# A decoder step on one core: second half's attention outputs of layer 1 kept in DRAM as fp32, and Winograd weight sums of layer 1 made by VectorE

## The chip, the core and the metric

The kernel runs on one core of one Trainium2 chip. The metric is the device time of one execution in microseconds, lower is better. Matrix products run on TensorE (PE in the profile; PEld are its weight loads), element-wise work on VectorE (DVE) and ScalarE (ACT), and DMAs are issued from the queues of SyncE (SP) and GpSimd (POOL).

## The reference, cut to what matters

A two-layer decoder trunk handles a prompt of 1024 tokens and eight sample tokens with the same weights (model width 1024, 4+4 heads of 128, feed-forward width 2816). Layer 0 mixes with a gated linear recurrence and attention into 256 memory tokens; layer 1 with stick-breaking attention over one shared K/V and memory attention. Each layer ends with a SwiGLU, and every sub-layer is normed on both sides:

```python
def swiglu(h, w_gu, w_down):
    gate, up = jnp.split(h @ w_gu, 2, axis=-1)
    return (jax.nn.silu(gate) * up) @ w_down
...
        else:
            mix = b_mixer(hn, w_in_b[l - N_A], sb_bias[l - N_A], k_all, v_all, q_pos, k_pos, ...)
        h = h + rmsnorm(mix, g[1])
        h = h + rmsnorm(swiglu(rmsnorm(h, g[2]), w_gu[l], w_down[l]), g[3])
```

Everything is fp32.

## The kernel before, in words

**Halves and precision.** The tokens are worked on in two halves: half 0 has 512 prompt tokens, half 1 has 512 and the eight sample tokens (520 columns). Activations lie transposed, 128 features on the partitions, tokens along the row; a half is eight such tiles `x[k]`. A fp32 product is made of three products of rounded parts: `split_to` (L226) and `split_w` (L192 on) write a high part with ScalarE (L206, L227) and the rest with VectorE (L207, L228). `proj` (L211) multiplies eight weight tiles of 128x128 with the eight `x[k]` into a bank of PSUM (L220).

**Plain and Winograd blocks.** The feed-forward width is cut into 22 blocks of 128, in five parts of 5, 5, 4, 4 and 4 (`PARTS`). For each part the gate and up products of its blocks come first, then its way down: eight row tiles (`w_down`), added to the result `R`. `ffn.part` does this plainly. `ffn_w` does it for half 1 of layer 1 (`f1`) and in two other places: its first blocks are plain too, with two banks per product (`gate_up_q`, L452 on, products L464), and beside them `sums_w` (L277 on) makes sums of `x` (L298, L306); its other blocks (`gate_up_w`, L481 on) need seven products of half the tokens and half the rows instead of eight, a Winograd scheme (products L511). Each of the seven needs one 512x128 weight, split at L501/L502; four of the seven weights are sums of two to four quarters of `w_gu`. For `f1` blocks 0 to 2 are plain and 19 are Winograd blocks. The products end in four PSUM banks, each held once, so a bank must be evacuated (L518 to L535) before the next block's product into it.

**Where the weight sums come from.** `weight_sums` (L545 on) forms four sums per part in DRAM with plain and accumulating DMAs of 256 rows from GpSimd's queue, 16 per part; a one-column copy (L563) holds each of them until the other work is as far as the weave wants. For layer 1 that is `ws`, 80 DMAs, woven into the stages from layer 0's memory attention on to the output projection of half 1. `gate_up_w` then loads each of the seven weights with one DMA (L496) from `w_gu` or from a sum.

**Order.** The work is written as generators that `weave` interleaves by given weights; what the tile framework makes of it is a fixed order on every engine, and each engine runs its own in that order. Buffers are taken from pools in turn (`wraw` 5 raw weights, `wspl` 5 split weights, `bpool` 7 rows of 512, `tpool` 3, `npool` 2). Towards the end the stages are:

1. Attention of half 1 in layer 1 (`b1.sb`, `b1.mem`, and the sample's attentions), woven with parts 0, 1, 2 of half 0's plain feed-forward and with the four gate/up steps of its part 3 (`p3`). Each head's output `po` is split into `xo[k]`, a tile with both parts (L912 and L1405); the sample's eight columns are added at L959.
2. The output projection of half 1, `o1.mm` (384 products), woven with the last `ws`.
3. `o1.finish`: norm (`rstd_from`, its products are L256), residual (L381, L387), a second norm, and `normed` (L273, L228), which makes the `x` of `f1`; woven with the rest of `p3`, its way down, and part 4.
4. `f1.part(0)` and `part(1)`, woven with the end of half 0 (`f0.finish`, also L381, L387, and the transposes of `store_y`, L1453), then parts 2, 3 and 4. The way down of `ffn_w` is L648 with its evacuations at L655 and L657.

Of the kernel before, what the change touches and what calls it, by code (L numbers as in the profile page):

```python
# [18 lines left out]
P = 128  # L19
# [4 lines left out]
def tile_decoder(  # L24
# [201 lines left out]
    def split_to(dst, src):  # L226
        nc.scalar.copy(dst[0], src)  # L227
        nc.vector.tensor_sub(dst[1], src, dst[0].bitcast(F32))  # L228

    def silu(dst, ps, g):  # L230
# [251 lines left out]
    def gate_up_w(g, l, f, ops, spl, raws):  # L482
# [4 lines left out]
        gate, up = f * P, DFF + f * P  # L487
        src = [
            (w_gu[l][0:512, gate : gate + P], 0), (sums[l][part][0][:, o : o + P], 4), (sums[l][part][1][:, o : o + P], 5),
            (w_gu[l][512:D, gate : gate + P], 1), (sums[l][part][2][:, o : o + P], 6), (sums[l][part][3][:, o : o + P], 2),  # L490
            (w_gu[l][512:D, up : up + P], 3),
        ]
# [12 lines left out]
        def product(ps, j, first=False):  # L505
            w = split(weight(j))
            i = src[j][1]
            for k in range(4):
# [66 lines left out]
    class ffn_w:  # L575
# [288 lines left out]
    def mem_attn(g, l, qm, xo):  # L864
# [4 lines left out]
        for h in range(H):  # L869
            po = S()  # L870
            for pr in range(2):
# [38 lines left out]
                yield  # L910
            d = xo[H + h]
            split_to((d[:, 0, :G], d[:, 1, :G]), po)  # L912

# [25 lines left out]
    def sample_pv(pT, load, xo, k0):  # L939
# [15 lines left out]
        for h in range(H):  # L955
            nc.tensor.transpose(pr[:, h * NB : (h + 1) * NB], ot[:NB, h * P : (h + 1) * P], ident[:NB, :NB])
        for h in range(H):
            d = xo[k0 + h]
            split_to((d[:, 0, G : G + NB], d[:, 1, G : G + NB]), pr[:, h * NB : (h + 1) * NB])  # L959
        yield  # L960
# [379 lines left out]
    def sb_prompt(g, Qs, xo):  # L1340
# [49 lines left out]
        for h in range(H):  # L1390
# [12 lines left out]
            values(vh, po, *late)  # L1403
            d = xo[h]
            split_to((d[:, 0, :G], d[:, 1, :G]), po)  # L1405

# [17 lines left out]
    class mixer_b:  # L1424
# [6 lines left out]

        def open(self):
            self.xo = wo_tiles(self.g)

# [117 lines left out]
    weave((a1.sample(), 6), (a1.gate(), 4), (f0.part(1), 9), (w0, 9))  # L1552
    ws = weight_sums(1, range(5))

# [8 lines left out]

    weave((chain(a1.merge(), a1.mem()), 30), (a1.mem_sample(), 50), (rest(), 24), (islice(ws, 2), 6))
    xk0, xb0 = [], []
# [6 lines left out]
    b0 = mixer_b(0, xb0)  # L1572
    weave((b0.heads(), 8), (o1.finish(), 17), (islice(ws, 4), 4))
    b0.open()
    f1 = ffn(1, 0, o1.x)
    weave((chain(b0.sb(), b0.mem()), 25), (chain(f1.part(0), f1.part(1)), 18), (islice(ws, 34), 35))
    set_banks(True)
    fw = ffn_w(1, 0, o1.x, (5, 6, 5), 2, False, f1.R)
    weave((chain(fw.part(2), fw.part(3), fw.part(4)), 24), (islice(ws, 8), 8))
    f1.acc = fw.acc  # L1580
# [5 lines left out]
    weave((normed(1, f1.R, f1.r, gkvcol, xk1, True), 8), (o0.mm(b0.xo, 5, 7), 2))  # L1586
    weave((kv_proj(1, xk1), 8), (islice(ws, 10), 11))
    weave((normed(1, f1.R, f1.r, lambda k: gcol(1, 0, k), xb1), 8), (o0.mm(b0.xo, 7, ND), 1))
    b1 = mixer_b(1, xb1)
    weave((b1.heads(), 8), (o0.finish(), 17), (islice(ws, 8), 9))  # L1590
    b1.open()
    f0 = ffn(0, 1, o0.x)
# [44 lines left out]
```

## Time and profile before

| | |
|---|---|
| timed runs | 2450.82 us median of 3 (2448.91 to 2453.11) |
| the profiled execution | 2446.43 us |
| its span, first to last instruction | 2444.6 us |
| mean granted TensorE clock | 0.999 |
| moved by DMA | 397.42 MB, mean 163 GB/s |
| the chain that ended last | PE 87%, DVE 6%, DMA 3%, rest under 3% each |

The page of the profile gives busy times for the whole span; stages are read from windows of it. A row of a window has the stretch, its length, then for each engine the busy time and the number of instructions, the granted clock, the share of the DMA engines and GB/s. A row of the groups has line, engine, operation, tiles, shapes and count, then busy time and mean ns of one, then the engine's idle time before them and what ended it. A row of the timeline has start, length, engine, line, operation, tiles and count, and in brackets the idle time before it. Line numbers are those of the kernel before; in the changed kernel they lie 8 to 45 lines later.

### The profile page before, as it was taken

Reading aid. Unit: us, or ns where it says so; the run is one execution under the profiler, and the core shown is the slowest. Engines: PE = TensorE matmul, PEld = TensorE weight load, DVE = VectorE, ACT = ScalarE, POOL = GpSimd, SP = SyncE. Lnnn points to the kernel's source line nnn. Section 1 sums busy time; section 2 is a strip of 40 time slices with the busy share of each in tenths; the row PEclk is TensorE's granted clock in tenths of the full one; section 3 lists DMA queues with packets and bytes.
Section 4 is the critical chain, followed back from the end, with each engine's and each line's share of the span. In section 5 each row is a group of like instructions: output and inputs, shape, how many; then the busy total and the mean of one; then the engine's idle time right before and its main releaser. Section 6 shows DMA issues by size and latency. Waiting matters only on the chain.

```text
span 2444.6 us, 42106 instructions
## 1 busy us (share of the span) xinstructions
PE 2412.0 (99%) x15839; PEld 2159.3 (88%) x15839; DVE 1639.0 (67%) x2987; ACT 1251.2 (51%) x2441; POOL 186.1 (8%) x315
## 2 busy tenths in 40 slices
PE   8999999999999999999999999999999999999998
PEld 6888888888889988999999989877777888999998
DVE  5867557665897686654756686777788467755565
ACT  5547544344445555554434554555555445654445
POOL 1001101101000000111200102121000100000000
PEclk9999999999999999999999999999999999999999
DMA  5454666577746447677766649655354563464542
GB/s 187 120 166 117 161 191 158 134 192 186 209 132 172 123 156 232 179 179 168 196 166 165 202 139 293 196 151 150 99 163 121 145 192 119 140 193 144 148 145 73
DMA packets 534734, 397.42 MB, mean 163 GB/s; under 512 B 21325, under 2 KB 473018, under 8 KB 534530
## 3 DMA queue, kind: packets, MB, share of 16 engines
q1 hardware_dynamic: 505346, 315.02, 43.3%
q0 software_dynamic: 29184, 79.70, 14.1%
q8 instruction: 125, 2.05, 0.3%
q14 instruction: 79, 0.65, 0.1%
HBM read 364.81 MB, written 101.14 MB: 191 GB/s over the span
## 4 chain that ended last, share of the span: by engine, by line
PE 87%; DVE 6%; DMA 3%; issue 2%; ACT 2%; POOL 0%; SPq 0%; DVEq 0%; ACTq 0%; POOLq 0%
PE mm L220 46%; PE q L511 13%; PE q L648 9%; PE q L464 3%; PE mm L1042 2%; PE s L1188 1%; PE s L906 1%; PE s L1385 1%; PE mm L851 1%; PE mm L824 1%; PE s L875 1%; PE q L680 1%; PE s L1351 1%; DVE ws L207 1%; DMA b<-qd 1%
## 5 line engine op out<-in xcount | busy, mean ns | idle before, releaser
L220 PE MATMUL mm<-x,ws 128*128 128x260 f32 (+1 forms) x6240 | 1115.6, 335 | 3.5 <-DVE r L657 1.7
L220 PEld LDWEIGHTS mm<-x,ws 128*128 128x128 f32 x6240 | 941.0, 188 | 123.9 <-DVE x L228 2.1
L206 ACT CAST ws<-w 128x512 fp32r<-128x512 f32 (+1 forms) x652 | 382.3, 588 | 492.1 <-PE mm L220 336.2
L207 DVE TENSOR_TENSOR ws<-w,ws 128x512 fp32r<-128x512 f32 (+1 forms) x652 | 418.6, 648 | 246.0 <-ACT ws L206 232.0
L220 PE MATMUL mm<-m,ws 128*128 128x512 f32 (+1 forms) x1344 | 281.8, 361 | 0.5 <-DVE r L400 0.4
L220 PEld LDWEIGHTS mm<-m,ws 128*128 128x128 f32 x1344 | 217.8, 188 | 37.2 <-issue 1.0
L648 PE MATMUL q<-m,ws 128*128 128x260 f32 (+1 forms) x1824 | 222.0, 282 | 0.0
L648 PEld LDWEIGHTS q<-m,ws 128*128 128x128 f32 x1824 | 219.0, 188 | 1.3 <-DVE t L534 0.7
L502 DVE TENSOR_TENSOR ws<-w,ws 128x512 fp32r<-128x512 f32 x181 | 124.0, 690 | 89.7 <-ACT ws L501 86.3
L501 ACT CAST ws<-w 128x512 fp32r<-128x512 f32 x181 | 111.8, 621 | 110.8 <-PE q L648 31.9
L511 PE MATMUL q<-x,ws 128*128 128x260 f32 (+1 forms) x1188 | 158.1, 282 | 0.0
L511 PEld LDWEIGHTS q<-x,ws 128*128 128x128 f32 x1188 | 148.7, 188 | 0.0
L511 PE MATMUL q<-y,ws 128*128 128x260 f32 x912 | 119.7, 283 | 0.4 <-ACT q L521 0.4
L511 PEld LDWEIGHTS q<-y,ws 128*128 128x128 f32 x912 | 113.6, 188 | 0.9 <-ACT q L521 0.6
L464 PE MATMUL q<-x,ws 128*128 128x260 f32 (+1 forms) x720 | 91.3, 284 | 0.2 <-DVE r L400 0.2
L464 PEld LDWEIGHTS q<-x,ws 128*128 128x128 f32 x720 | 88.4, 188 | 1.8 <-DVE r L400 0.5
L511 PE MATMUL q<-a,ws 128*128 128x260 f32 (+1 forms) x672 | 87.0, 282 | 0.0
L511 PEld LDWEIGHTS q<-a,ws 128*128 128x128 f32 x672 | 83.2, 188 | 0.0
L657 DVE TENSOR_TENSOR r<-r,q 128x260 f32<-128x260 f32 (+1 forms) x128 | 48.4, 420 | 48.2 <-PE q L648 48.1
L237 DVE TENSOR_SCALAR t<-mm 128x512 f32<-128x512 f32 (+1 forms) x58 | 40.0, 690 | 48.6 <-PE mm L220 48.4
L563 POOL COPY mk<-a 128x1 f32<-128x1 f32 x36 | 21.9, 609 | 640.4 <-ACT a L1241 392.1
L566 POOL DMA_DIRECT2D wsum<-in_w_gu x64 | 58.5, 935 | 114.1 <-DMA wsum<-wsum 89.5
(355 smaller groups left out, 3027.8 us busy)
## 6 DMA issues: line engine op xcount, KB each, us to landing
w<-in_w_gu SPq DMA_DIRECT2D x297, 256.0 KB
w<-in_w_down SPq DMA_DIRECT2D x160, 256.0 KB
wsum<-in_w_gu POOLq DMA_DIRECT2D x72, 512.0 KB, 6.5
w<-wsum SPq DMA_DIRECT2D x104, 256.0 KB
w<-in_w_in_a SPq DMA_DIRECT2D x80, 256.0 KB
w<-in_w_o SPq DMA_DIRECT2D x64, 256.0 KB
wsum<-in_w_gu POOLq DMA_DIRECT2D x24, 640.0 KB, 6.8
wsum<-wsum POOLq DMA_DIRECT2D x24, 512.0 KB, 5.6
```

Source lines behind the costliest of these rows:

```text
L206: nc.scalar.copy(ws[:, 0, :n, :], raw[:, :n, :])
L207: nc.vector.tensor_sub(ws[:, 1, :n, :], raw[:, :n, :], ws[:, 0, :n, :].bitcast(F32))
L220: nc.tensor.matmul(ps[:, a, : PW[g]], wt, xt[k][:, xi, o : o + PW[g]], start=(k == 0 and wi == 0), stop=(k == nk - 1 and wi == 2),)
L237: nc.vector.tensor_scalar(sv(x, g), pv(ps, g), -44.0, None, op0=ALU.max)
L464: ins = nc.tensor.matmul(pp[a][:, :h], wt, xt[k][:, xi, a * h : (a + 1) * h], start=(k == 0 and wi == 0), stop=(k == ND - 1 and wi == 2),)
L501: nc.scalar.copy(w[:, 0, :], src)
L502: nc.vector.tensor_sub(w[:, 1, :], src, w[:, 0, :].bitcast(F32))
L511: nc.tensor.matmul(ps[:, :h], w[:, wj, k * P : (k + 1) * P], x[:, xi, :], start=(first and k == 0 and wi == 0), stop=(k == 3 and wi == 2), ...
L566: nc.gpsimd.dma_start(d, a, accum_op=ALU.add)
L648: nc.tensor.matmul(pp[a][:, :h], wt, mids[k][:, xi, a * h : (a + 1) * h], start=(k == 0 and wi == 0), stop=(k == nf - 1 and wi == 2),)
L657: nc.vector.tensor_add(d, d, pp[a][:, :h])
L1042: nc.tensor.matmul(pb[i][:, a, :], xt[k][:, xi, c * P : (c + 1) * P], ws[:, s, :], start=(k == 0 and wi == 0), stop=(k == ND - 1 and wi == 2),
```

## The change

Three things, all for layer 1.

- `b1.open(True)` makes `xo` one fp32 DRAM tensor. A head's output goes there through a `b` buffer (`put`: a copy by ScalarE and a DMA), the sample's columns with one DMA. `b1.load()` reads the eight tiles back into `t` buffers and splits them into `x` tiles.
- The order at the end of half 0: the way down of `p3` is woven with `b1.load()` ahead of `o1.mm`; `o1.finish` is woven with part 4 alone.
- `weight_sums(1, ...)` is not called. `gate_up_w` without sums loads the four quarters a11, a21, a22, a12 at the start of a block and makes the sums with four `tensor_add` on VectorE. Raw weights of part 0 alternate with `b` buffers.

```diff
+    def put(xo, i, cols, src):
+        if isinstance(xo, list):
+            split_to((xo[i][:, 0, cols], xo[i][:, 1, cols]), src)
+            return
+        t = B()[:, : cols.stop - cols.start]
+        nc.scalar.copy(t, src)
+        nc.sync.dma_start(xo[:, i, cols], t)
...
         def weight(j):
-            r = raws()
-            nc.sync.dma_start(r, src[j][0].rearrange("(k p) m -> p k m", p=P))
-            return r.rearrange("p k m -> p (k m)")
+            if src:
+                return load(src[j][0])
+            if j == 0:
+                for name, r, c in (("a11", 0, gate), ("a21", 0, up), ("a22", 512, up), ("a12", 512, gate)):
+                    raw[name] = load(w_gu[l][r : r + 512, c : c + P])
+            elif j == 1:
+                raw["s1"] = B()
+                nc.vector.tensor_add(raw["s1"], raw["a21"], raw["a22"])
+            elif j == 2:
+                nc.vector.tensor_add(raw["a21"], raw["a11"], raw["a21"])
+                raw["s2"] = B()
+                nc.vector.tensor_add(raw["s2"], raw["a21"], raw["a22"])
+            elif j == 5:
+                nc.vector.tensor_add(raw["s2"], raw["s2"], raw["a12"])
+            return raw[("a11", "s1", "s2", "a12", "a21", "s2", "a22")[j]]
...
+            if self.rows and not self.pi and self.r % 2:
+                return B().rearrange("p (k m) -> p k m", k=4)
...
-            d = xo[H + h]
-            split_to((d[:, 0, :G], d[:, 1, :G]), po)
+            put(xo, H + h, slice(0, G), po)
...
+        else:
+            t = small([P, H * NB], tag="ss")
+            nc.scalar.copy(t, pr[:, : H * NB])
+            nc.sync.dma_start(xo[:, k0 : k0 + H, G : G + NB], t.rearrange("p (h b) -> p h b", h=H))
...
+        def load(self):
+            d, n, self.xo = self.xo, NG[self.g], []
+            ts = []
+            for k in range(ND + 2):
+                if k < ND:
+                    ts.append(T()[:, :n])
+                    nc.sync.dma_start(ts[k], d[:, k, :n])
+                if k >= 2:
+                    x = X(self.g)
+                    split_to((x[:, 0, :n], x[:, 1, :n]), ts[k - 2])
+                    self.xo.append(x)
+                yield
...
-    ws = weight_sums(1, range(5))
...
-    b1.open()
+    b1.open(True)
...
     o1 = out_proj(1, 1, A, True)
-    weave((o1.mm(b1.xo), 8), (ws, 9))
-    weave((o1.finish(), 17), (chain(p3, f0.part(4, True)), 12))
+    weave((p3, 4), (b1.load(), 10))
+    drain(o1.mm(b1.xo))
+    weave((o1.finish(), 17), (f0.part(4, True), 8))
```

The `islice(ws, ...)` streams are also taken out of the earlier weaves.

More of the change, by code (lines that the diff above doesn't have):

```diff
@@ L487, in gate_up_w @@
         gate, up = f * P, DFF + f * P
-        src = [
+        src = None if l not in sums else [
             (w_gu[l][0:512, gate : gate + P], 0), (sums[l][part][0][:, o : o + P], 4), (sums[l][part][1][:, o : o + P], 5),
@@ L956, in sample_pv @@
             nc.tensor.transpose(pr[:, h * NB : (h + 1) * NB], ot[:NB, h * P : (h + 1) * P], ident[:NB, :NB])
-        for h in range(H):
-            d = xo[k0 + h]
-            split_to((d[:, 0, G : G + NB], d[:, 1, G : G + NB]), pr[:, h * NB : (h + 1) * NB])
+        if isinstance(xo, list):
+            for h in range(H):
+                put(xo, k0 + h, slice(G, G + NB), pr[:, h * NB : (h + 1) * NB])
+        else:
+            t = small([P, H * NB], tag="ss")
+            nc.scalar.copy(t, pr[:, : H * NB])
+            nc.sync.dma_start(xo[:, k0 : k0 + H, G : G + NB], t.rearrange("p (h b) -> p h b", h=H))
         yield
@@ L1430, in heads, with open @@
             yield from heads2(self.g, w_in_b[0], 4 * P, self.xt, scaled_evac, A, self.Qm)
-        def open(self):
-            self.xo = wo_tiles(self.g)
+        def open(self, dram=False):
+            self.xo = tc.dram_tile([P, ND, WID], F32, name=nm("xo")) if dram else wo_tiles(self.g)
+        def load(self):
[10 more added lines that the diff above has]
+                yield
         def sb(self):
@@ L1562, in rest @@
         set_banks(False)
-    weave((chain(a1.merge(), a1.mem()), 30), (a1.mem_sample(), 50), (rest(), 24), (islice(ws, 2), 6))
+    weave((chain(a1.merge(), a1.mem()), 30), (a1.mem_sample(), 50), (rest(), 24))
     xk0, xb0 = [], []
@@ L1572, in tile_decoder @@
     b0 = mixer_b(0, xb0)
-    weave((b0.heads(), 8), (o1.finish(), 17), (islice(ws, 4), 4))
+    weave((b0.heads(), 8), (o1.finish(), 17))
     b0.open()
     f1 = ffn(1, 0, o1.x)
-    weave((chain(b0.sb(), b0.mem()), 25), (chain(f1.part(0), f1.part(1)), 18), (islice(ws, 34), 35))
+    weave((chain(b0.sb(), b0.mem()), 25), (chain(f1.part(0), f1.part(1)), 18))
     set_banks(True)
     fw = ffn_w(1, 0, o1.x, (5, 6, 5), 2, False, f1.R)
-    weave((chain(fw.part(2), fw.part(3), fw.part(4)), 24), (islice(ws, 8), 8))
+    drain(fw.part(2), fw.part(3), fw.part(4))
     f1.acc = fw.acc
@@ L1586, in tile_decoder @@
     weave((normed(1, f1.R, f1.r, gkvcol, xk1, True), 8), (o0.mm(b0.xo, 5, 7), 2))
-    weave((kv_proj(1, xk1), 8), (islice(ws, 10), 11))
+    drain(kv_proj(1, xk1))
     weave((normed(1, f1.R, f1.r, lambda k: gcol(1, 0, k), xb1), 8), (o0.mm(b0.xo, 7, ND), 1))
     b1 = mixer_b(1, xb1)
-    weave((b1.heads(), 8), (o0.finish(), 17), (islice(ws, 8), 9))
-    b1.open()
+    weave((b1.heads(), 8), (o0.finish(), 17))
+    b1.open(True)
     f0 = ffn(0, 1, o0.x)
```

10 lines of the change are left out of this document (7 added, 3 removed).

## The prediction

> **What bounds the kernel now.** First the page's head and the busy shares, then the stages around the edits (columns of the second fence: stretch, length, busy time and instructions of each engine, granted clock, DMA share, GB/s).
>
> ```profile
> span 2444.6 us, 42106 instructions
> PE 2412.0 (99%) x15839; PEld 2159.3 (88%) x15839; DVE 1639.0 (67%) x2987; ACT 1251.2 (51%) x2441; POOL 186.1 (8%) x315
> ```
>
> ```profile
> 1550.00:1930.00 380.00, 373.00 (x1759) 288.69 (x1758) 286.13 (x448) 198.14 (x383) 26.05 (x24) 1.00 0.45 137
> 1930.00:1976.00 46.00, 46.00 (x385) 45.91 (x384) 15.89 (x24) 17.82 (x32) 13.98 (x28) 1.00 1.00 257
> 1976.00:2027.50 51.50, 51.46 (x222) 40.89 (x221) 35.80 (x56) 26.21 (x43) 0.02 (x1) 1.00 0.44 126
> 2027.50:2103.00 75.50, 75.43 (x466) 67.26 (x465) 65.76 (x127) 44.38 (x78) 0.00 (x0) 1.00 0.36 109
> 2103.00:2128.00 25.00, 24.57 (x203) 23.79 (x202) 18.66 (x36) 16.44 (x36) 0.00 (x0) 1.00 0.68 200
> 2161.00:2211.00 50.00, 50.00 (x419) 50.00 (x418) 31.26 (x57) 30.16 (x65) 0.00 (x0) 1.00 0.64 180
> 2211.00:2240.00 29.00, 29.00 (x244) 28.85 (x243) 15.68 (x35) 9.29 (x20) 0.00 (x0) 1.00 0.39 114
> 2436.00:2444.60 8.60, 1.79 (x15) 1.37 (x14) 2.73 (x4) 1.70 (x6) 0.00 (x0) 0.73 0.31 124
> ```
>
> TensorE is busy in 2412.0 of 2444.6 us, and the change alters none of its products, only their order. So no stage can give back more than its few idle microseconds: 7.0 of 380 in the attention stage (first row), nothing in the output projection (second row), even with DMA at 1.00. What can happen is that another engine falls behind. VectorE is nearest to that in the fourth row: 65.76 of 75.5 us, while TensorE loses nothing. That stage lies between the two edits, so I read its order of products.
>
> ```profile
> 1918.02 0.41 PE L956 MATMUL s<-ident,b 8*128 8x8 f32 x4
> 1975.53 3.43 PE L220 MATMUL mm<-m,ws 128*128 128x512 f32 x14
> 1999.09 22.36 PE L220 MATMUL mm<-x,ws 128*128 128x512 f32 x96
> 2024.20 0.39 PE L256 MATMUL ns<-n,onesr 128*128 128x8 f32 x2
> 2024.44 20.12 PE L220 MATMUL mm<-x,ws 128*128 128x512 f32 x86
> 2044.40 22.42 PE L220 MATMUL mm<-m,ws 128*128 128x512 f32 x96
> 2066.66 3.50 PE L464 MATMUL s<-x,ws 128*128 128x260 f32 x28
> 2092.13 11.29 PE L464 MATMUL q<-x,ws 128*128 128x260 f32 x92
> 2103.25 1.60 PE L511 MATMUL q<-x,ws 128*128 128x260 f32 x12
> 2128.10 7.41 PE L648 MATMUL q<-m,ws 128*128 128x260 f32 x60
> ```
>
> At 1975.5 the output projection ends and the way down of part 3 begins (96 products). L256 at 2024.2 ends the second norm of `o1.finish`. After it TensorE has 86 products of gate and up, part 4's way down (96), three plain blocks (L464) and at 2103.25 the first Winograd block (L511); the way down of part 0 follows at 2128.1.
>
> **The change, part by part.**
>
> *Part 3's way down goes ahead of the output projection.* The built order of the changed kernel has 96 products, then the 384 of the projection, then all 192 gate and up products of part 4, the second norm, part 4's way down and the plain blocks. The norm stays where it is relative to the projection's end (96+96 products before, 192 now). Behind it 96 products are missing: 22.3 us (2044.4 to 2066.7). From the norm's end (2024.6) to the first Winograd block TensorE had 78.7 us and now has 56.4. What must VectorE do in that time?
>
> ```profile
> L207 DVE TENSOR_TENSOR ws<-w,ws 128x512 fp32r<-128x512 f32 x22 | 14.8, 686 | 4.9 <-ACT ws L206 4.9
> L306 DVE TENSOR_TENSOR b<-b,b 128x260 f32<-128x260 f32 x16 | 6.7, 422 | 0.0
> L298 DVE TENSOR_TENSOR b<-x 128x260 f32<-128x260 f32 x16 | 6.2, 422 | 0.0
> L273 DVE SCALAR_TENSOR_TENSOR n<-a,par,st 128x520 f32<-128x520 f32 x8 | 6.0, 755 | 1.3 <-ACT st L258 1.3
> L381 DVE SCALAR_TENSOR_TENSOR r<-r,par,st 128x512 f32<-128x512 f32 x8 | 5.9, 742 | 0.5 <-ACT st L258 0.5
> L228 DVE TENSOR_TENSOR x<-n,x 128x520 fp32r<-128x520 f32 x8 | 5.5, 695 | 0.1
> L228 DVE TENSOR_TENSOR y<-b,y 128x260 fp32r<-128x260 f32 x14 | 5.5, 421 | 0.3 <-ACT y L227 0.3
> L400 DVE TENSOR_TENSOR r<-r,mm 128x512 f32<-128x512 f32 x8 | 5.5, 683 | 1.9 <-PE mm L220 1.9
> L387 DVE TENSOR_TENSOR r<-r,ht 128x512 f32<-128x512 f32 x8 | 5.4, 681 | 0.0
> L267 DVE TENSOR_TENSOR st<-st,n 128x512 f32<-128x512 f32 x7 | 4.8, 685 | 0.2 <-ACT n L266 0.2
> L477 DVE TENSOR_TENSOR t<-t,q 128x260 f32<-128x260 f32 x4 | 1.6, 417 | 0.0
> ```
>
> ```profile
> 2027.84 1.43 DVE L273 SCALAR_TENSOR_TENSOR n<-a,par,st 128x520 f32<-128x520 f32 x2 [1.26 <-ACT st L258]
> 2094.22 1.44 DVE L298 TENSOR_TENSOR b<-x 128x260 f32<-128x260 f32 x4
> 2106.36 2.49 DVE L502 TENSOR_TENSOR ws<-w,ws 128x512 fp32r<-128x512 f32 x4
> ```
>
> These groups are 2027.5 to 2103. Neighbours on VectorE overlap: four L298 of 0.42 take 1.44 us, so one starts (1.44-0.42)/3 = 0.34 us after the other; four 512-wide ones (0.69) take 2.49, so 0.60. Likewise 0.67 for L273 and 0.66 for L381. In the changed order there stand, from the first L273 to the first weight split of the first Winograd block: 8 at 0.67, 8 at 0.66, 45 at 0.60 (13 weight splits, 10 splits of x and m, 7 L267, 6 evacuations, 7 residual adds, the norm's split, the first L502) and 50 at 0.34 (16+16+14 for the sums of x, 4 multiplications). That is 5.4+5.3+27.0+17.0 = 54.7 us.
>
> Now both engines by hand, from the norm's end as zero. L273 began 3.2 us after it (2027.84); now two evacuations and a split stand ahead of it that need the second tile of the way down (3.3 us), so it begins at 4.7. VectorE, never idle, is at the first Winograd split at 59.4; TensorE, never waiting, is there at 54.9 (19.9 for the way down, 288 products at 11.29/92 = 0.12). But they also wait for each other. The second weights of the first plain block stand 22.7 us down VectorE's queue, at 27.9 (4.7+22.7, and half a microsecond in which squares and normed rows wait for the two `n` buffers they share); TensorE wants them at 24.2 and ends the block at 35.8. VectorE's multiplication for this block was due at 33.8 and waits those 2 us; the third block adds half a microsecond likewise, and the last multiplication ends with TensorE. So the first Winograd block begins at about 64.5, **9.6 late**. In the two Winograd blocks of part 0 VectorE had 18.66 of 25 us and gets eight sums (8 at 0.60 = 4.8): nearly full, but TensorE no longer loses what it lost there (the second weight comes 1 us late, the last evacuation 1.7). I come to the way down of part 0 at 89.0. Before it was 103.5 after the norm (2128.1); less the 22.3, 81.2. **Sum: +7.8 us.** Below: 0, if VectorE's queue is reordered or idles less; 4.5 without any mutual waiting; above: 13, if each hand-over between engines costs half a microsecond more.
>
> *The sums of layer 1's weights on VectorE.* 76 additions (4 for 19 blocks) of the form of L267: 0.60 us back to back, 45.8 in all. Five blocks take 50 us and 31.26 of VectorE; with 20 sums it has 43.3. Each way down (29 us, 15.68) has room. The changed order puts the weights of about seven products (10 us) ahead of TensorE, so the late evacuations are covered. +0.5 us, between 0 and +8 (half a microsecond in each of the 17 other blocks, if a sum stands ahead of an evacuation that TensorE waits for). The four loads of a block now come first; SyncE's queue holds them while a buffer is taken, about one and a half blocks (15 us) ahead. For the second Winograd block they stand behind two stores of `y_prompt`, which wait for transposes that follow the first block's first product; they go out near 68 on the clock above and are wanted at 75. If they land later than that, the difference is lost once.
>
> *80 accumulating DMAs of POOL go.*
>
> ```profile
> wsum<-in_w_gu POOLq DMA_DIRECT2D x72, 512.0 KB, 6.5
> PE s L1380 <- ACT b L1374: 2.1, 3, 1.4
> PE s L1385 <- ACT b L1382: 1.9, 2, 1.5
> PE s L1351 <- DVE b L1366: 1.4, 2, 1.0
> ```
>
> TensorE waits for none of them; the projection ran through at DMA share 1.00. 0, between -1 and 0.
>
> *Attention outputs through DRAM.* In the attention stage (last three rows: its waits) VectorE loses 8 splits of 512 columns (4.8 us) and 8 tiny ones, of 286 us; ScalarE keeps a copy, which takes one of seven `b` buffers until its DMA has landed. -0.5, between -7 (all idle time of the stage) and +3 (buffers). The splits come back beside part 3's way down: 8 of 520 columns, with 8 evacuations and 8 weight splits some 15 us of VectorE in 22. The last sample output leaves TensorE at 1918 (L956), and the projection, which began 384 products of 0.12 before 1975.5, near 1929.5, now begins 22.3 later, near 1952: 33 us for a write, reads and splits. The nearest row, POOL's trip from DRAM to DRAM, lands in 6.5 us; twice that and 10 us of splits is 23. Hidden: 0. The eight reads stand on SyncE's queue between the last loads of part 3's way down and those of the projection's weights, and each waits there for one of three `t` buffers; if a read takes 6.5 us like POOL's, three rounds are 20 us and hold those weights up by some 3: +3 at most. [...]
>
> Together 7.8+0.5+0-0.5 = **+7.8 us**. The profiled execution took 2446.43 us with a span of 2444.6; the median of the three timed runs is 2450.82. I take the difference as equal for both kernels: **2458.6 us**.
>
> **The rivals.**
>
> 1. *VectorE's lateness does not reach TensorE.* For it: in the fourth row it ran 65.76 of 75.5 with TensorE untouched. Against: then 22.3 us more of products lay beside it. It costs 0 to 4: 2447 to 2455.7, about 2452.
> 2. *The attention stage gives more than the late stage takes* (the other side). Place: the waits of L1380, L1385 and L1351 behind the chain of `sb_prompt`, which shares VectorE with the removed splits. Price: up to the 7.0 idle us. It needs the late stage near 0, since +7.8 outweighs all of it; from there it decides once more than 4.9 of the 7.0 come back: about 2444. Against: the waits named sum to 5.4, and most are for ScalarE, which does no less.
> 3. *VectorE bounds the Winograd blocks.* 43.3 of 50 us is an average; if a sum delays the evacuation of `pb`, each block loses half a microsecond: 17 at 0.5 = 8.5 more, 2467.
> 4. *The waits pull the clock down.* In the last stretch TensorE is mostly idle and the granted clock is 0.73; everywhere else here it is 1.00. My longest new waits are 3.7 and 2.6 us. If the clock were 0.73 after them for as long as they lasted, 6.3*(1/0.73-1) = 2.3 us more: 2461. [...]
>
> **How the numbers follow.** A measurement of this kernel can tell about 0.2% (4.9 us) from no change. Chances: the forecast, with rival 4 near it (2455.7 to 2464): 0.58; rival 1: 0.20; rival 2: 0.07; rival 3, or the late stage at its upper bound (2464 to 2475): 0.15. So slower 0.73, same 0.20, faster 0.07. The range leaves out most of rival 2 and the end of rival 3: 2448 to 2470.
>
> **What would show it.** In the changed profile, between the second norm's L256 and part 0's way down: VectorE without gaps until the first Winograd block, TensorE waiting there some 10 us for weight splits, sums of x and sums of weights, hardly any before. The Winograd blocks of parts 1 to 4 at 10 us each with VectorE near 43 of 50. The projection beginning without a wait for `x`. Wrong would be: no waits in that stage (rival 1), blocks over 10.3 us (3), a granted clock below 1 (4), or an attention stage shorter by more than 5 us (2).

## The result, and the profile after

The changed kernel takes 2455.15 us (median of 20 runs, 2452.22 to 2456.64); the kernel before, run beside it, 2449.10 us (20 runs, 2447.03 to 2454.11). The ratio is 1.0019, 95% interval 1.0013 to 1.0026: 4.7 us more, between 3.2 and 6.4 (the two medians lie 6.1 apart, inside that interval). The forecast was +7.8 us, 2458.6 in a range of 2448.0 to 2470.0. The sign was right and the size too large; of the terms behind it some were right and some were not, as the sections below show. Of the bands to which the prediction gave chances, 2455.15 lies half a microsecond below the forecast's own (2455.7 to 2464) and in that of rival 1 (2447 to 2455.7), so the time alone doesn't tell the two apart. The waits do: rival 1 said that VectorE's lateness does not reach TensorE, and it does.

The profiled execution took 2456.08 us. First its head, then its stages; the rows have the columns of those shown of before. The third row reaches from the end of the second norm to the first Winograd block, the fourth holds the Winograd blocks of part 1.

```profile
span 2454.1 us, 41788 instructions
PE 2414.2 (98%) x15839; PEld 2160.2 (88%) x15839; DVE 1682.3 (69%) x3054; ACT 1254.3 (51%) x2443; POOL 95.6 (4%) x155
```

```profile
1500.00:1550.00 50.00, 49.70 (x394) 48.26 (x393) 40.43 (x68) 27.85 (x49) 0.00 (x0) 1.00 0.60 184
1550.00:1900.00 350.00, 341.92 (x1624) 264.33 (x1624) 265.80 (x409) 182.59 (x352) 26.50 (x24) 1.00 0.49 143
2047.90:2109.90 62.00, 58.87 (x386) 53.58 (x386) 58.89 (x117) 37.58 (x67) 0.00 (x0) 0.97 0.29 82
2166.70:2219.50 52.80, 50.80 (x423) 50.59 (x422) 38.65 (x71) 30.07 (x65) 0.00 (x0) 1.00 0.36 106
```

The same stretches of the kernel before, where they were not shown yet:

```profile
1500.00:1550.00 50.00, 49.70 (x394) 48.30 (x393) 40.47 (x68) 27.30 (x48) 15.27 (x16) 1.00 0.98 281
1550.00:1900.00 350.00, 343.00 (x1626) 264.67 (x1625) 271.38 (x422) 184.24 (x357) 26.05 (x24) 1.00 0.47 141
2160.90:2211.30 50.40, 50.40 (x422) 50.40 (x421) 31.66 (x57) 30.28 (x65) 0.00 (x0) 1.00 0.64 181
```

Read them pairwise. The attention stage has lost 5.6 us of VectorE's work (271.38 to 265.80) and TensorE has not gained: it is idle 8.1 us of 350 instead of 7.0. Part 1 is 2.4 us longer, and TensorE is idle for 2.0 of them, though VectorE with its sums is busy in only 38.65 of 52.8 us. And in the third row TensorE is idle 3.1 us where it had no gap before.

Now the order of TensorE's products after the second norm (L264), as far as it waits. Gaps stand in brackets.

```profile
2047.52 0.39 PE L264 MATMUL ns<-n,onesr 128*128 128x8 f32 x2
...
2067.73 4.46 PE L472 MATMUL s<-x,ws 128*128 128x260 f32 x36
...
2075.68 8.88 PE L472 MATMUL q<-x,ws 128*128 128x260 f32 x72 [0.43 <-DVE ws L207]
...
2086.12 0.33 PE L1497 MATMUL s<-ident,r 128*128 128x128 f32 x1 [1.45 <-DVE r L395]
2086.72 0.33 PE L1497 MATMUL s<-ident,r 128*128 128x128 f32 x1 [0.28 <-DVE r L395]
2087.32 9.80 PE L472 MATMUL q<-x,ws 128*128 128x260 f32 x68 [0.27 <-DVE ws L207]
...
2097.84 0.75 PE L472 MATMUL q<-x,ws 128*128 128x260 f32 x4 [0.61 <-DVE t L485]
...
2109.92 1.61 PE L538 MATMUL q<-x,ws 128*128 128x260 f32 x12
...
2133.90 7.42 PE L677 MATMUL q<-m,ws 128*128 128x260 f32 x60
```

Against before, by the times of the two traces, the plain blocks begin 1.1 us late (2067.73, was 2066.66), the first Winograd block 6.7 (2109.92, was 2103.25) and the way down of part 0 5.8 (2133.90, was 2128.10). Counted from the norm's end (2047.9; before 2024.6, with 22.3 us of products that have moved away), the stage has lost 86.0-81.2 = 4.8 us. Part 1 then loses 2.4 and the rest about 1.7; TensorE's last product ends 9.9 us later.

These 9.9 us are those of two single executions (2446.43 and 2456.08 us). That of before lies 2.7 below its median of 20, that of after 0.9 above, so 3.6 us of the difference are the choice of executions. Every size below is therefore read inside a stage, and what an edit is worth in all is taken from the ratios.

### The profile page after: what moved, and what is told of

Same layout as the page of the kernel before. It is cut to its first block, busy times and chain, and to the rows that moved or that the text cites. A ratio compares the mean times of both kernels' runs of the same rounds, so it can differ in the third digit from the quotient of the medians.

```text
span 2454.1 us, 41788 instructions
## 1 busy us (share of the span) xinstructions
PE 2414.2 (98%) x15839; PEld 2160.2 (88%) x15839; DVE 1682.3 (69%) x3054; ACT 1254.3 (51%) x2443; POOL 95.6 (4%) x155
## 4 chain that ended last, share of the span: by engine, by line
PE 83%; DVE 8%; DMA 3%; issue 3%; ACT 2%; POOL 0%; SPq 0%; POOLq 0%; DVEq 0%; ACTq 0%
PE mm L220 45%; PE q L538 13%; PE q L677 8%; PE q L472 2%; PE mm L1074 2%; PE s L1220 1%; PE s L935 1%; PE s L1417 1%; PE mm L880 1%; PE mm L853 1%; DVE ws L207 1%; PE q L709 1%; DMA c<-in_cache_mem_v 1%; PE s L904 1%; PE s L1383 1%
## 5 line engine op out<-in xcount | busy, mean ns | idle before, releaser
L538 PE MATMUL q<-x,ws 128*128 128x260 f32 (+1 forms) x1188 | 158.1, 282 | 0.0
L538 PEld LDWEIGHTS q<-x,ws 128*128 128x128 f32 x1188 | 148.7, 188 | 0.0
L538 PE MATMUL q<-y,ws 128*128 128x260 f32 x912 | 120.3, 284 | 2.6 <-DVE t L556 2.0
L538 PEld LDWEIGHTS q<-y,ws 128*128 128x128 f32 x912 | 113.7, 188 | 3.5 <-DVE t L556 2.2
L529 DVE TENSOR_TENSOR ws<-w,ws 128x512 fp32r<-128x512 f32 x120 | 82.2, 689 | 39.9 <-ACT ws L528 37.7
L528 ACT CAST ws<-b 128x512 fp32r<-128x512 f32 x111 | 68.7, 621 | 69.8 <-PE q L677 32.6
L528 ACT CAST ws<-w 128x512 fp32r<-128x512 f32 x120 | 74.1, 622 | 59.2 <-PE q L538 21.5
L529 DVE TENSOR_TENSOR ws<-b,ws 128x512 fp32r<-128x512 f32 x111 | 76.2, 689 | 31.0 <-ACT ws L528 29.4
L538 PE MATMUL q<-a,ws 128*128 128x260 f32 (+1 forms) x672 | 87.0, 282 | 0.0
L538 PEld LDWEIGHTS q<-a,ws 128*128 128x128 f32 x672 | 83.2, 188 | 0.0
L686 DVE TENSOR_TENSOR r<-r,q 128x260 f32<-128x260 f32 (+1 forms) x128 | 48.4, 420 | 35.2 <-PE q L677 35.0
```

What stands on the lines that cost most here:

```text
L528: nc.scalar.copy(w[:, 0, :], src)
L529: nc.vector.tensor_sub(w[:, 1, :], src, w[:, 0, :].bitcast(F32))
L538: nc.tensor.matmul(ps[:, :h], w[:, wj, k * P : (k + 1) * P], x[:, xi, :], start=(first and k == 0 and wi == 0), stop=(k == 3 and wi == 2), ...
L686: nc.vector.tensor_add(d, d, pp[a][:, :h])
```

## The experiments

Line numbers in this section are those of the kernel in question; the changed kernel's L538 (Winograd products), L556 (evacuation of `pb`), L517 (first sum) and L529 (splits) move by a few lines.

| kernel | what it is | median, us | ratio to before, 95% interval |
|---|---|---|---|
| order_only | before, with part 3's way down ahead of the projection | 2452.63 | 1.0011 (1.0002 to 1.0020) |
| sums_only | the change without DRAM trip and order | 2450.74 | 1.0007 (0.9997 to 1.0016) |
| xo_only | the change with the sums left in DRAM | 2452.53 | 1.0019 (1.0010 to 1.0028) |
| norm_early6 | the change, second norm 48 products earlier | 2450.71 | 1.0004 (0.9995 to 1.0013) |
| norm6_behind2 | norm_early6, first sum queued behind an evacuation | 2445.39 | 0.9989 (0.9980 to 0.9998) |
| trip_bare | the change with the order of before | 2454.15 | 1.0025 (1.0015 to 1.0034) |
| sums_pool | the change, sums made by GpSimd | 2477.05 | 1.0121 (1.0105 to 1.0136) |
| norm_late12 | the change, second norm some 61 products later | 2461.67 | 1.0057 (1.0038 to 1.0075) |
| behind2 | the change, first sum queued behind an evacuation | 2449.49 | 1.0008 (0.9998 to 1.0017) |
| sums_behind2 | sums_only, first sum queued behind an evacuation | 2444.63 | 0.9987 (0.9978 to 0.9996) |
| bare_behind2 | trip_bare, first sum queued behind an evacuation | 2448.98 | 1.0005 (0.9996 to 1.0014) |
| dma_kept | sums_behind2 with the 80 DMAs of before issued as well | 2446.74 | 1.0000 (0.9991 to 1.0010) |

The theory: the late stage loses because the 96 products that lay beside VectorE's norm work are gone. Its rivals: the sums on VectorE bound it (A), or the trip through DRAM costs (B).

### Which of the edits costs: order_only, sums_only, xo_only

order_only is the kernel before with

```diff
+    drain(p3)
     weave((o1.mm(b1.xo), 8), (ws, 9))
-    weave((o1.finish(), 17), (chain(p3, f0.part(4, True)), 12))
+    weave((o1.finish(), 17), (f0.part(4, True), 8))
```

> The kernel before with only the order at the end of half 0 changed: part 3's way down goes ahead of the output projection, as in the changed kernel; the attention outputs stay on the chip and the weight sums stay in DRAM. Theory (cover): the changed kernel loses most in the stage between the second norm and the way down of part 0, because 96 products (22.3 us) that lay beside VectorE's norm work are gone; so this edit alone costs 3 to 5 us, seen as waits of L1464-like plain blocks and transposes between the norm and the first Winograd block. Rival A (sums on VectorE): about 0, since VectorE has no sums. Rival B (DRAM trip): 0.

Ratio 1.0011, 2.7 us (0.5 to 4.9), a little under the 3 to 5 expected. TensorE's waits from 2040 to 2140 us (waiter, releaser, total, times, longest):

```profile
PE s L1453 <- DVE r L387: 1.7, 2, 1.4
PE q L464 <- DVE ws L207: 0.7, 2, 0.4
PE q L464 <- ACT c L1456: 0.6, 1, 0.6
```

The same products wait for the same times as in the changed kernel, without a sum on VectorE and without a trip through DRAM: the late stage's loss belongs to the order alone. From the norm's end (2048.6) to the way down of part 0 (2133.2) it takes 84.6 us, 3.4 more than before.

sums_only takes the other side, the changed kernel with `b1.open()` and the old two lines of order.

> The changed kernel with the attention outputs on the chip and the order of before: only the weight sums are made by VectorE. Theory (cover): the stage after the second norm has its 96 products again and loses under 1 us; what stays is the wait of about 2 us at the second Winograd block of part 1, where a sum waits for a weight load ahead of an evacuation, and some waits of half a microsecond: +2 to +3 us in all. Rival A (sums on VectorE bound it): +5 or more, with the waits in the late stage still there. Rival B (DRAM trip): 0 to +1.

Ratio 1.0007, 1.7 us, the interval from -0.7 to 3.9; 2 to 3 were expected. The late stage has no wait (way down of part 0 at 2127.5, before 2128.1). What remains is the wait in part 1, here 3.04 us at 2172.34. So rival A falls for the late stage; the sums do cost, but elsewhere.

xo_only is the changed kernel with `weight_sums(1, ...)` and the DMA loads of before.

> The kernel before with the attention outputs through DRAM and the changed order, the weight sums staying in DRAM. Theory (cover): the same as the order alone, +3 to +5 us, with no wait of the output projection for its x tiles. Rival A: about 0. Rival B (the trip through DRAM or its splits cost): more than the order alone by 2 us or more.

Ratio 1.0019, within the 3 to 5 us expected. The late stage has the waits of order_only, and part 1 is 50.4 us long (2167.1 to 2217.5), as before. The ratio lies 2 us above order_only's, which is just what rival B asked for, but the intervals overlap. This pair does not decide; norm_early6, and norm6_behind2 beside sums_behind2, do so below.

### The cover beside the second norm: norm_early6 and norm_late12

In the changed kernel VectorE had done all that the second norm needs by 2030.7, and the norm stood behind all 192 gate and up products of part 4, at 2044.6. One number moves it:

```diff
-    weave((o1.finish(), 17), (f0.part(4, True), 8))
+    weave((o1.finish(), 17), (f0.part(4, True), 6))
```

> The changed kernel with one number altered: the norm work of o1.finish is woven with part 4 by 17 to 6 instead of 17 to 8, so the second norm stands after 144 products of part 4 instead of 192 and 48 products (11.1 us) more lie beside VectorE's work behind it. Nothing is left out. Theory (cover): the late stage's waits of TensorE go, 4 to 5 us less than the changed kernel, so within 2 us of before. Rival A (VectorE's total work bounds the stage) and rival B: the same as the changed kernel, about +5 against before.

Ratio 1.0004, 3.7 us below the changed kernel's by the ratios. In the traces, from the start of the projection to the way down of part 0, it takes 175.3 us (1951.32 to 2126.64) and the changed kernel 180.7 (1953.25 to 2133.90), 5.3 less. The first Winograd block begins at 2102.7 and the way down of part 0 at 2126.6, with no wait of TensorE in between but 0.2 us. The waits of the late stage are gone with VectorE's sums and the trip left as they were: the theory's point, and rivals A and B fall there.

norm_late12 has 12 in that place.

> The changed kernel with the norm work woven 17 to 12 instead of 17 to 8: the second norm stands after 192 products of gate and up and 71 of part 4's way down, so some 61 products (14 us) fewer lie behind it than in the changed kernel. Nothing is left out. Theory (cover): VectorE's work behind the norm is the same and TensorE waits for it that much longer: 12 to 15 us more than the changed kernel, and more if the waits are long enough for the granted clock to fall. Rival (the waits are caused by single hand-overs and not by the missing products): 0 to 4 us more.

Ratio 1.0057 from two runs (1.0038 to 1.0075): by the ratios some 9 us more than the changed kernel, with an uncertainty of about 5. The same stretch of the trace takes 186.6 us (1951.17 to 2137.81), 6.0 more than in the changed kernel; some more is lost in part 1, where the wait is 2.85 us instead of 2.00 and the clock is 0.57 for 3.4 us behind it. The direction is the theory's; in the stage that it speaks of the size is half of the 12 to 15 expected. "The same work behind the norm" was wrong. When products move ahead of the norm, their weight splits and evacuations move with them. Counted in the traces from the first normed row (L281) to the first split of a Winograd weight (L529), VectorE executes 110 instructions ahead of that split in the changed kernel, 98 in norm_late12 and 119 in norm_early6; the 50 short ones are the same, and each of the others takes 0.60 back to back. So 14 us less cover came with 12 instructions (7.2 us) less work, 7 us net; and 11.1 us more with 9 more (5.4), 5.7 net. The traces have 6.0 and 5.3: moving the norm is worth about half of the products moved.

### A sum ahead of an evacuation: norm6_behind2, behind2, sums_pool

In part 1 of the changed kernel TensorE waits once for 2 us. TensorE's row, then VectorE's rows just before it:

```profile
2177.50 1.71 PE L538 MATMUL q<-y,ws 128*128 128x260 f32 x12 [2.00 <-DVE t L556]
```

```profile
2172.81 0.70 DVE L517 TENSOR_TENSOR b<-w,w 128x512 f32<-128x512 f32 x1 [2.22 <-DMA w<-in_w_gu]
...
2177.03 0.42 DVE L556 TENSOR_TENSOR t<-t,q 128x260 f32<-128x260 f32 x1
```

L556 evacuates `pb` of the part's first block, f=5, whose product ends at about 2174. Ahead of it on VectorE stands L517, the first sum of block f=8, three blocks further on, and that waits 2.22 us for a weight: SyncE issued its loads of weights at that time between 2168.2 and 2170.4, as splits (L529) freed the buffers. VectorE then works off seven sums and splits, that one included, before it comes to L556. Before the change nothing of VectorE's was that far ahead: each weight came with a load of its own, and of the work on weights only splits stand ahead of this evacuation, in both kernels the same twelve of blocks 5 and 6.

norm6_behind2 changes this order and nothing else of norm_early6:

```diff
-                nc.vector.tensor_add(raw["s1"], raw["a21"], raw["a22"])
+                with tc.issue_after(evacs[-2].ins) if len(evacs) > 1 else nullcontext():
+                    nc.vector.tensor_add(raw["s1"], raw["a21"], raw["a22"])
...
-        nc.vector.tensor_add(gt[:, h:n], dt[:, h:n], pb[:, :h])
+        ev = nc.vector.tensor_add(gt[:, h:n], dt[:, h:n], pb[:, :h])
+        if not src:
+            evacs.append(ev)
```

> The kernel norm_early6 with one more edit: the first weight sum of a Winograd block is queued on VectorE behind the evacuation of pb (L556 of the changed kernel) two blocks before, so that its wait for a weight load no longer stands ahead of the evacuation that TensorE needs. Nothing is left out. Theory: the wait of 2.8 us in part 1 and the products at 0.215 us that follow it both go; 4 us less than norm_early6 in part 1, and within 1 us of before in all. Rival (VectorE has too much work for the blocks in any order): the wait moves to another place of the part and the time stays.

Ratio 0.9989, interval 0.9980 to 0.9998: 2445.39 us, 3.7 less than norm_early6 by the ratios, as expected, and 2.7 less than before, where I had expected to come within 1. The evacuation (L557 here) runs on time, and TensorE has no wait in the blocks of part 1:

```profile
2167.21 0.42 DVE L557 TENSOR_TENSOR t<-t,q 128x260 f32<-128x260 f32 x1
```

The rival, that the wait moves elsewhere in the part, falls. behind2 is the changed kernel with that edit alone.

> The changed kernel with only the first weight sum of a Winograd block queued behind the evacuation of pb two blocks before; the second norm stays where the change put it. Nothing is left out. Theory: the wait in part 1 goes (2.2 us in the profile of the changed kernel), the late stage still loses 4 to 6 us; so 2 to 3 us less than the changed kernel, 4 to 6 us more than norm6_behind2, ratio to before 1.0005 to 1.0020. Rival (the queueing alone brings what norm6_behind2 brought): ratio 0.999 to 1.000.

Ratio 1.0008, as the theory had it. The late stage still has the waits of 0.7, 1.7 and 0.6 us, part 1 has none. By the ratios the queueing alone brings 2.7 us, the early norm alone 3.7, and both together 7.3: within their uncertainty the two losses add up.

sums_pool makes the sums with `nc.gpsimd.tensor_add`.

> The changed kernel with the 76 weight sums made by GpSimd instead of VectorE. Theory: the late stage loses its 5 us all the same, because VectorE's norm work lacks the 96 products; the wait in part 1 shrinks or moves, because a weight load no longer holds VectorE ahead of the evacuation: 0 to 4 us less than the changed kernel, unless GpSimd is slower than TensorE needs (four sums in 10 us) or slows VectorE. Rival A (the sums bound VectorE in the late stage too): 5 us or more less, with the late waits gone.

Ratio 1.0121: 30 us slower than before, which neither theory had. The late stage loses what it lost (waits of 0.7, 1.7 and 0.6 us again), but now TensorE waits in the blocks as well: 5.6 us for L556, 5.0 for L548 and 2.5 for a split (L529), where the changed kernel has 2.0 for L556 and 0.6 for the way down (L686). By my reading what it waits for stands behind GpSimd's sums. GpSimd's rows, then VectorE's beside them:

```profile
2162.34 1.29 POOL L517 TENSOR_TENSOR b<-w,w 128x512 f32<-128x512 f32 x1 [36.28 <-DMA w<-in_w_gu]
2163.71 1.64 POOL L519 TENSOR_TENSOR w<-w,w 128x512 f32<-128x512 f32 x1
2172.46 1.82 POOL L521 TENSOR_TENSOR b<-w,w 128x512 f32<-128x512 f32 x1
```

```profile
2172.46 2.38 DVE L529 TENSOR_TENSOR ws<-w,ws 128x512 fp32r<-128x512 f32 x2
2174.76 0.68 DVE L529 TENSOR_TENSOR ws<-b,ws 128x512 fp32r<-128x512 f32 x1
```

A sum takes GpSimd 1.29 to 1.82 us in these rows, where VectorE takes 0.69 (L517 of the changed kernel, mean of 17). Two splits of VectorE beside the sum at 2172.46 take 2.38 instead of the 1.28 that such a pair takes in the changed kernel, about half a microsecond more for each, while the next, alone, takes 0.68. What makes them longer beside a sum was not shown.

### The trip through DRAM: trip_bare, bare_behind2, sums_behind2

trip_bare has nothing moved beside the trip:

```diff
-    weave((p3, 4), (b1.load(), 10))
+    drain(b1.load())
     drain(o1.mm(b1.xo))
-    weave((o1.finish(), 17), (f0.part(4, True), 8))
+    weave((o1.finish(), 17), (chain(p3, f0.part(4, True)), 12))
```

> The changed kernel with nothing beside the trip of the attention outputs through DRAM: the reads and splits stand directly ahead of the output projection, and part 3's way down is woven with o1.finish as before. TensorE's wait ahead of the projection measures what the 22.3 us of the way down have to hide. [...] The late stage loses nothing, as the 96 products are back. Rival (DRAM trip costs more than the cover): over 22 us.

TensorE waited far less than the 8 to 20 us that I had worked out from 13 us for a write and a read (twice the 6.5 us of GpSimd's DMAs) and up to 10 us of splits, as 48 products that I had overlooked still stand beside the trip. (The 6.5 us are those of DMAs issued by GpSimd; these are SyncE's, and no run shows the landing time of one.) TensorE's rows from the last sample output (L984, which ends at 1919.2) on:

```profile
1919.09 14.54 PE L220 MATMUL mm<-x,ws 128*128 128x512 f32 x70
1933.90 1.97 PE L220 MATMUL mm<-x,ws 128*128 128x260 f32 x14 [0.27 <-ACT x L227]
1936.55 2.35 PE L220 MATMUL mm<-x,ws 128*128 128x260 f32 x15 [0.68 <-ACT x L227]
1939.30 20.90 PE L220 MATMUL mm<-x,ws 128*128 128x260 f32 x166 [0.40 <-ACT x L227]
```

Three waits, 1.35 us together. With many short ones TensorE is some 4 us above its pace between 1900 and 1950, against 0.1 in sums_only; its pace is the usual time from the start of one product to the next, 0.232 us with 512 columns and 0.120 with 260. The 48 products left of a gate and up step (11.1 us) cover most of the trip. So the 22.3 us of the way down, which the change moved there, hid some 4 us, and cost 3 to 5 at the place they were taken from. The ratio (1.0025) is no better than the change's; part 1's wait is there as well (2.1 us).

bare_behind2 takes that wait out of trip_bare; sums_behind2 takes it out of sums_only, which has no trip at all.

> The kernel trip_bare (attention outputs through DRAM with only the 48 products left of the way down step beside the trip, 96 products back beside the norm) with the first weight sum queued behind the evacuation two blocks before. Nothing is left out. Theory: the trip costs TensorE its 2.5 to 3 us ahead of the projection and nothing else is lost: 2 to 3 us more than norm6_behind2, ratio to before 0.9995 to 1.0005, and less than the changed kernel. Rival: the reads also hold up the projection's weights, and the ratio is over 1.001.

> The kernel sums_only (order of before, attention outputs on the chip) with the first weight sum queued behind the evacuation two blocks before. Nothing is left out. Theory: no wait in part 1 and none in the late stage; like norm6_behind2, ratio 0.998 to 1.000: the sums on VectorE then cost nothing, and the trip through DRAM brings nothing either. Rival (the trip through DRAM, by taking splits out of the attention stage, brought norm6_behind2 its 2 us): ratio 1.000 to 1.001 here.

1.0005 and 0.9987. The first lies at the upper edge of what the theory had, 3.9 us above norm6_behind2 instead of 2 to 3; it is 4.4 above sums_behind2, which is again the price of the trip without the way down beside it. The second is as the theory had it: sums_behind2 does without the trip and is as fast as norm6_behind2 (0.9989, with trip, way down and early norm). So the trip gains nothing, and well covered it costs nothing (rival B). Its part 1 is 50.5 us long, part 2 40.5; with the sum queued behind the evacuation, VectorE's sums cost TensorE next to nothing there (50.4 and 40.3 before).

### What the DMAs cost: dma_kept

Open was why two of these kernels are 2 to 3 us below before. dma_kept issues the DMAs again and uses VectorE's sums all the same (`src = None if l == 1`, and `ws` woven as before).

> The kernel sums_behind2 with GpSimd's 80 plain and accumulating DMAs of layer 1's weight sums issued as in the kernel before, though nothing reads what they write; the Winograd blocks still use VectorE's sums. Open is why sums_behind2 and norm6_behind2 are 2 to 3 us below before, when the profile of before shows no wait of TensorE for these DMAs. The times of the kernels that issue them scatter by about 2 us (standard deviation), those without by 0.6 to 1.5. Theory: the DMAs delay TensorE a little in some executions; with them back the ratio is 0.9995 to 1.0005 and the scatter about 2 us. Rival: they are free, as the prediction costed them, and the gain comes from the blocks themselves: ratio 0.998 to 0.9992 and a scatter near 1 us.

Ratio 1.0000 (0.9991 to 1.0010), scatter 2.5 us against 1.2 for sums_behind2: the theory's figures, though the intervals of the two kernels, which ran on different chips, overlap, and the difference may be anything from 0 to 6 us. The scatter by itself tells little: norm_early6 issues none of these DMAs and scatters by 2.0. The traces show one place where the DMAs cost something. TensorE's row at the start of the attention stage in before, dma_kept, xo_only, and then sums_behind2 (four kernels, one line each):

```profile
1553.60 1.14 PE L1351 MATMUL s<-a,a 128*128 128x128 f32 x4 [0.70 <-DMA a<-ksc]
```

```profile
1554.78 1.14 PE L1386 MATMUL s<-a,a 128*128 128x128 f32 x4 [1.44 <-DMA a<-ksc]
```

```profile
1556.10 1.14 PE L1381 MATMUL s<-a,a 128*128 128x128 f32 x4 [2.65 <-DMA a<-ksc]
```

```profile
1553.59 1.03 PE L1386 MATMUL s<-a,a 128*128 128x128 f32 x4
```

The wait is for a load of K; the share of the DMA engines just before is 0.98 in before and 0.60 in the changed kernel (the rows for 1500 to 1550 above). All four traces with the accumulating DMAs have this wait (order_only's is 0.8 us), none of the ten without has it. That it makes up the whole 2 to 3 us is not shown: the profiled executions of dma_kept and sums_behind2 are equally long (2446.49 and 2446.81 us; the second is the slowest of its kernel), and the others left no trace.

## Why the prediction was right, and where it was not

*What bounds the kernel; products unchanged.* Right: all 15839 products remain. TensorE's idle time grew from 32.6 to 39.9 us, and its busy time by 2.2 us.

*Part 3's way down ahead of the projection: +7.8.* The mechanism was right (order_only, norm_early6); the size was 4.8, of which 1.3 are the clock's (below). VectorE's tally (111 instructions with the split that ends it, 54.7 us) was right: L281 begins 4.7 us after the norm, as worked out, and the first Winograd split follows 56.3 us later.

```profile
2052.58 0.76 DVE L281 SCALAR_TENSOR_TENSOR n<-a,par,st 128x520 f32<-128x520 f32 x1
...
2092.28 0.43 DVE L228 TENSOR_TENSOR y<-b,y 128x260 fp32r<-128x260 f32 x1 [1.43 <-ACT y L227]
...
2108.84 0.68 DVE L529 TENSOR_TENSOR ws<-b,ws 128x512 fp32r<-128x512 f32 x1
```

The step that failed is "they also wait for each other": I let the multiplications hold VectorE until TensorE had ended the block, 5 us in all, and put the first Winograd block at 64.5. VectorE waited 1.7 us, nearly all of it in the 1.43 above, which is for a split by ScalarE; none of the four multiplications (L485) waited, and the block began at 62.0. Nor do two figures of the working fit together: 54.9 for TensorE leaves out transposes and norm products that stand between, for the rows give 56.4. So "9.6 late" is 8.1 against before, of which 5.6 came; the sum was taken from 81.2 and isn't touched by it. And the waits fell elsewhere than I said: 1.7 of the 3.1 us at the transposes of `store_y` (L1497), which wait for residual adds that I had counted as work of VectorE without asking who waits for them. None was for sums of x or of weights, for which the prediction had expected some.

*The granted clock (rival 4).* It was put inside the forecast's range, at 2.3 us. The waits that it was priced for, of 3.7 and 2.6 us, did not come, but the clock fell all the same, and not by the length of a wait. Changed kernel and order_only have the same waits at the same products; in each, the row of the waits and the four microseconds behind them:

```profile
2084.40:2088.00 3.60, 1.60 (x8) 0.98 (x7) 3.60 (x7) 1.21 (x3) 0.00 (x0) 0.86 0.00 0
2088.00:2092.00 4.00, 4.00 (x26) 4.00 (x26) 2.85 (x8) 1.17 (x5) 0.00 (x0) 0.70 0.68 195
```

```profile
2085.10:2088.70 3.60, 1.60 (x10) 1.03 (x9) 3.60 (x7) 1.19 (x3) 0.00 (x0) 1.00 0.00 0
2088.70:2092.70 4.00, 4.00 (x35) 4.00 (x35) 3.96 (x12) 1.92 (x5) 0.00 (x0) 1.00 0.65 180
```

At 0.70 TensorE gets through 26 products instead of 35: 13 of them at 0.217 instead of 0.120 us, 1.3 us. So of the 4.8 us of the late stage 1.3 are the clock's, in this execution; order_only, where the clock stayed, lost 3.4. Why the same waits were followed by the lower clock in one execution and not in the other was not shown. Here it fell at about 2087.0, behind waits of 1.45 and 0.28 us that stand close together.

*The sums: +0.5, and rival 3.* Wrong in size and place: 2.4 us in part 1 in this execution, and some of the 1.7 lost behind it. The mechanism was named for rival 3 ("if a sum delays the evacuation of `pb`"), but at half a microsecond in each of 17 blocks; it is one wait of 2 to 3 us, where the sum ahead of the evacuation itself waits 2.22 us for a weight, and a third of a microsecond at three later places. The prediction's sign of rival 3, blocks over 10.3 us, did come in part 1 (52.8 us for five), but not in part 2 (40.5 for four). In some traces the clock falls behind this wait too: after norm_early6's 2.7 us it is 0.50 for 3.3 us.

```profile
2171.30:2174.60 3.30, 3.27 (x15) 3.27 (x16) 2.12 (x5) 0.64 (x2) 0.00 (x0) 0.50 0.60 169
```

VectorE's share was not the cause: it is 38.65 of 52.8 us, below the 43.3 of 50 forecast because eight of the part's 20 sums were made before it began, and in sums_behind2 the same sums cost next to nothing.

*80 DMAs of POOL go: 0, between -1 and 0.* Too narrow. TensorE does not wait for these DMAs themselves, but in the four traces that have them it waits 0.7 to 2.65 us for a load of K, and in the ten that don't it doesn't; with dma_kept against sums_behind2 the saving is some 3 us by the ratios, anywhere between 0 and 6. I asked who waits for these DMAs and not whose transfers they hold up.

*Attention outputs through DRAM: -0.5, hidden.* Hidden it is: the projection begins without a wait at 1953.25.

```profile
1953.25 49.31 PE L220 MATMUL mm<-x,ws 128*128 128x260 f32 x398
```

But the -0.5 did not come (rival 2 is out): with 5.6 us less on VectorE, TensorE is idle 1.1 us more in the stage. The prediction's price of 6.5 us for a DMA of SyncE was taken from GpSimd's; what the runs show is that some 15 us beside the trip (11.1 of products and 4 of waits, trip_bare) were enough. The largest new wait there is this one, for VectorE's scaling in the memory attention, which stands behind a load of `cache_mem_v` for the sample:

```profile
1884.59 0.30 PE L928 MATMUL s<-ident,b 128*128 128x128 f32 x1 [1.62 <-DVE b L921]
```

From the first product of the stage (the K row above) to the last sample output, the nine traces with the trip through DRAM take 363.7 to 366.0 us, the five without it 363.4 to 364.9. The two groups overlap, so neither a gain nor a loss is shown for the stage as a whole. What brings the new wait was not tried.

*In sum.* By the ratios the change is made of three parts: sums on VectorE in a good order and no accumulating DMAs, -3.2 us (sums_behind2, 0.9987); order and trip, +5.1 (behind2, 1.0008, against it); the sum ahead of the evacuation, +2.7 (1.0019 against behind2): +4.7 together, each with an uncertainty of 2 to 3 us. The forecast had 0, +7.3 and +0.5 for them. The saving that it missed (3.2) and the largest term (2.2 too large) both made it too high, and the wait in part 1 (2.2 more than forecast) took some of that back: that the total came within 3.1 us is in part luck.

## What to carry to other kernels

When products are moved to cover a transfer, work out what they covered where they stood: here 22 us of cover hid some 4 us of a trip, and their absence cost 3 to 5. An element-wise instruction that itself waits for a load should not stand in an engine's queue ahead of an evacuation that TensorE needs; ordering it behind that evacuation made 76 added sums next to free (sums_behind2: 50.5 and 40.5 us for parts 1 and 2, 50.4 and 40.3 before). A DMA that nobody waits for can still have a price: where the accumulating DMAs were issued, TensorE waited 0.7 to 2.65 us for a load of K that it did not wait for without them.

## What the runs showed of the hardware that I had not expected

The same 2.0 us of waits within 3.6 us, at the same products, were followed by a granted clock of 0.70 in one trace and of 1.00 in another. Longer waits do not decide it either: behind the 2.65 us shown above for xo_only it stayed at 1.00 (the four microseconds after them, first row), behind 2.03 us in norm_late12 it fell to 0.58 (the wait and the four microseconds after it).

```profile
1556.10:1560.10 4.00, 4.00 (x20) 3.09 (x21) 2.65 (x7) 1.27 (x2) 0.00 (x0) 1.00 1.10 351
```

```profile
2098.00:2100.10 2.10, 0.09 (x1) 0.00 (x0) 2.10 (x5) 0.19 (x2) 0.00 (x0) 1.00 0.00 0
2100.10:2104.10 4.00, 3.71 (x16) 3.38 (x17) 4.00 (x10) 1.79 (x4) 0.00 (x0) 0.58 0.19 57
```

The falls shown here and for norm_early6 slowed 13 to 15 products by some 0.1 us each, 1.3 to 1.5 us. They may be a reason why norm_early6 (2447.2 to 2453.1) scatters more than norm6_behind2 (2443.7 to 2446.2), which has no such wait; that was not tried.
